# Encoder trunk on one core: weight sums queued behind the normed operands, the mixer's evictions before its third operands, gates without GpSimd

## The chip, the cores and the metric

The kernel runs on one core of a Trainium2 chip. The metric is the device time of one launch in microseconds (us), the median of several runs. Lower is better.

## The reference

Two layers work on one sequence of 512 tokens with 1024 channels, all in float32. Each layer adds half a SwiGLU feed-forward stage, a token mixer and another half feed-forward stage to `x`, each behind an RMS norm:

```
x = x + 0.5 * swiglu(rmsnorm(x), w1_a, w3_a, w2_a)      # (silu(h @ w1) * (h @ w3)) @ w2, 2816 wide
h = rmsnorm(x); p = h @ w_in                            # fourier, B, C, v, pool: 512 each; gates 3 x 1024
x = x + (sig(g_f)*fourier(p_f) + sig(g_c)*conv(p) + sig(g_p)*pool(p_p)) @ w_o
x = x + 0.5 * swiglu(rmsnorm(x), w1_b, w3_b, w2_b)
```

`fourier` is the real part of a two-dimensional Fourier transform over tokens and over groups of 128 channels, followed by a linear map per group. `conv` is a gated convolution of width 3, `pool` a pooling over four window sizes with a linear map per group. A last norm makes the output.

## The kernel before, in words

**Products.** All activations lie transposed: 128 channels on the partitions, 512 tokens in the free dimension, eight such tiles for `x`. Every float32 product is three matmuls (`mm`, L354 to L358): both operands are split into a high and a low part of a reduced type (`h` and `l` at a name's end), and high x high (L356), high x low (L357) and low x high (L358) are added in PSUM. Making such a pair is a copy of the high part, on ScalarE as a rule, and a subtraction for the low part.

**Jobs of seven products.** Gate and up projections, and most of the mixer's input projection, are done as jobs of two output blocks with seven block products instead of eight: M1 to M7, each 4 x 3 matmuls of 256 columns. The activations' operands for them come from `operands(j)` (L452 to L481), called for j = 0 to 3, that is for pairs of `x` tiles. It makes two normed tiles `t` (L457: x times gain times `rstd`), four sums of 256 columns (L463 to L466, made by `tt`, whose instructions stand at L431), copies as high parts (L471, L476) and four low parts `n`. Two low parts are subtractions on VectorE (L478, which also shows as `n<-t,n` at L431). The two others are a negated copy on ScalarE (L473) and a DMA from GpSimd's queue that adds the source on top (L474). M1 needs what L471 and L478 make of the first unit, M5 and M7 the first accumulating DMA's result, M6 and M4 the second's.

**Weights.** `Weights` (L147) streams the weights in, as `Layout` planned it from a dry run: every step has a due time a fixed stretch ahead of its use (`AHEAD`), and is issued when the program's own estimate of time passes it. A load is a DMA on SP's queue (L185) into `raw` (3 buffers), `z` (2) or `w22` (2). For a job, `raw` holds the first blocks, `z` and `w22` the others. The steps are: `raw`, split with an accumulating DMA (L204 to L206); `sums`, two additions of 512 columns (L228, L229) and a split (L191 copy, L192 subtraction); `rest`, a subtraction of 1024 columns (L235) and a split, after which `raw` and `z` are free for the next load; and `last`, a split of `w22`. Subtractions of splits are held back in `tail` and issued by `finish` (L197).

**Stages.** A feed-forward stage begins with `lead` (L592): its first three hidden blocks (four in the first stage) are computed directly from the unscaled `h`, while the norm's factor `rstd` and the operands for the jobs are made; `gate_up` (L441) ends such a block with a multiplication by `rstd` on VectorE, a silu on ScalarE (L444), a second multiplication by `rstd` on GpSimd (`ptt`, L434), the product with the up projection (L431) and a split. The other blocks are jobs, run by `run` (L508), with pieces of the down projection between them.

**The mixer** (`mix`, L803) first does the small products of the Fourier map and the w_in product for the Fourier columns: four sums in PSUM, one per 128 tokens, whose last steps end one after another. `evict` (L822) copies each from PSUM, scaled: `pfh` on ScalarE (L825) and `pfl` on VectorE (L826). The operands 0 to 2 are made at steps 11, 17 and 23 of that loop, the last after it. Then `pf` is multiplied with the tables of the Fourier transform; the eight results are copied out as `half` (L859), four from each of two groups, and their banks in PSUM (eight in all) are used again by the jobs that follow. `join` (L739) combines two halves on VectorE.

**Order.** The program's text gives the order of tracing; the tile framework's scheduler then orders each engine's queue by when things can be ready, with the tracing order as the priority. Every engine works through its queue in that order and waits where its next instruction isn't ready. `tc.issue_after(i)` adds an order without a wait for data: what is traced inside stands behind instruction i in its engine's queue.

Of the kernel before, what the change touches and what calls it, by code (L numbers as in the profile page):

```python
# [1 line left out]

# [1 line left out]

# [6 lines left out]
F32 = mybir.dt.float32  # L11
F32R = mybir.dt.float32r
AF = mybir.ActivationFunctionType
ALU = mybir.AluOpType
# [46 lines left out]
NOTHING = Nothing()  # L61


class Order:


    def __init__(self):
        self.log, self.t = [], 0.0

    def start(self, x):  # L70
        pass
# [75 lines left out]
class Weights:  # L147
# [2 lines left out]

    BUFS = {"raw": 3, "z": 2, "w22": 2, "part": 6, "part22": 1}

    def __init__(self, nc, dram, pool, layout):
        self.nc, self.dram, self.pool, self.plan = nc, dram, pool, layout
        self.at, self.loads, self.splits = 0, list(layout.loads), list(layout.splits)
        self.used = dict.fromkeys(self.BUFS, 0)
        self.raws, self.ready, self.tail, self.t = {}, {}, [], 0.0
# [38 lines left out]

    def finish(self, t):  # L197
        while self.tail and self.tail[0][0] <= t:
            self.tail.pop(0)[2]()

    def added_parts(self, src, key, w=2 * S, tag="part"):

        hi, lo = (self.tile_of(tag, w if tag == "part22" else MAXW, F32R, tag + n) for n in "hl")
        self.nc.scalar.activation(lo[:, :w], src, AF.Copy, scale=-1.0)  # L204
        self.nc.gpsimd.dma_start(lo[:, :w], self.source(key), accum_op=ALU.add)  # L205
        self.nc.scalar.copy(hi[:, :w], src)  # L206
        return hi, lo

    def step(self, kind, key):
        v = self.nc.vector  # L210
# [41 lines left out]
    def advance(self, need):  # L252
        t = self.t = self.plan.log[self.at][2]
        self.finish(t - 1.3)
        while True:
            moved = False
            while self.loads and self.loads[0][0] <= t and self.load():
                moved = True
            while self.splits and self.splits[0][0] <= t and self.step(*self.splits[0][1:]):
                self.splits.pop(0)  # L260
                moved = True
            if not moved:
                break
        while need not in self.ready:
            if self.loads and self.load():
                continue
            assert self.step(*self.splits[0][1:]), (need, self.splits[0], self.used)
            self.splits.pop(0)
        if self.tail and any(made == need for _, made, _ in self.tail):
            self.finish(t)  # L270
# [30 lines left out]
def encoder(ctx: ExitStack, tc: tile.TileContext, layout, x_in, w_in, consts_in, gain_in, out):  # L301
    nc = tc.nc
    const = ctx.enter_context(tc.tile_pool(name="const", bufs=1))
    wpool = ctx.enter_context(tc.tile_pool(name="wpool", bufs=2))
# [1 line left out]
    tmp = ctx.enter_context(tc.tile_pool(name="tmp", bufs=2))  # L306
    psp = ctx.enter_context(tc.tile_pool(name="psp", bufs=8, space=bass.MemoryType.PSUM))

    weights = layout if isinstance(layout, Order) else Weights(nc, w_in, wpool, layout)
    cst = const.tile([P, NCONST[0]], F32, name="cst")  # L310
    nc.scalar.dma_start(cst, consts_in)
    zero = act.tile([P, S], mybir.dt.bfloat16, tag="act", name="zero")
# [47 lines left out]
    def cut(pair, a, b):  # L360
        return pair[0][:, a:b], pair[1][:, a:b]

    state = {}
# [66 lines left out]
    def tt(out, a, b, op=ALU.mult):  # L430
        nc.vector.tensor_tensor(out=out, in0=a, in1=b, op=op)  # L431

    def ptt(out, a, b, op=ALU.mult):
        nc.gpsimd.tensor_tensor(out=out, in0=a, in1=b, op=op)  # L434

    def t32(tag, w=S):

        wide = tag in ("t0", "t1", "t2", "t3")
        return tmp.tile([P, S + 32 if wide else S], F32, tag=tag, name=tag, bufs=1 if wide else 2)[:, :w]

    def gate_up(p1, p3):  # L441
        a = t32("a")
        tt(a, p1, state["r"])
        nc.scalar.activation(a, a, AF.Silu)  # L444
        ptt(a, a, state["r"])
        b = t32("b")
        tt(b, p3, a)
        pair = act_pair("g")
        split_tile(b, *pair)
        return pair  # L450

    def operands(j):  # L452


        w1, w2, z1, z2 = (act.tile([P, AW], F32, tag="act", name="t")[:, :S] for _ in range(4))
        for odd, w in enumerate((w1, w2)):
            nc.vector.scalar_tensor_tensor(  # L457
                out=w, in0=x[2 * j + odd], scalar=state["gain"][2 * j + odd], in1=state["r"],
                op0=ALU.mult, op1=ALU.mult,
            )  # L460

        left, right = slice(0, Q), slice(Q, S)
        tt(z1[:, left], w1[:, right], w1[:, left], ALU.subtract)  # L463
        tt(z1[:, right], w2[:, right], w1[:, right], ALU.subtract)
        tt(z2[:, left], w2[:, right], z1[:, left], ALU.subtract)
        tt(z2[:, right], w2[:, left], z2[:, left], ALU.subtract)  # L466
        units = [act.tile([P, AW], F32R, tag="act", name="n")[:, :S] for _ in range(7)]
        pairs = [units[0:2], units[2:4], units[4:6], (units[6][:, :Q], units[6][:, Q:])]
        sources = [w2, z1, z2, w1[:, left]]
        for i in (3, 0):  # L470
            nc.scalar.copy(pairs[i][0], sources[i])  # L471
        for i in (1, 2):
            nc.scalar.activation(pairs[i][1], sources[i], AF.Copy, scale=-1.0)  # L473
            nc.gpsimd.dma_start(pairs[i][1], sources[i], accum_op=ALU.add)  # L474
        for i in (1, 2):
            nc.scalar.copy(pairs[i][0], sources[i])  # L476
        for i in (3, 0):
            tt(pairs[i][1], sources[i], pairs[i][0].bitcast(F32), ALU.subtract)  # L478
        place = {"M1": (3, 0), "M2": (0, 0), "M3": (0, 1), "M5": (1, 0), "M7": (1, 1), "M6": (2, 0), "M4": (2, 1)}
        ops = {q: cut(pairs[i], h * Q, (h + 1) * Q) for q, (i, h) in place.items()}  # L480
        state.setdefault("n", []).append(ops)  # L481
# [321 lines left out]
    def mix(l, after):  # L803
# [31 lines left out]
        for n, (k, t) in enumerate(order):  # L835
            if n == 5:
                mean_squares(True)
            if n == 9:
                spread(True)
            if n in (11, 17, 23):  # L840
                operands((n - 11) // 6)
            if k == len(ws):
                ws.append(weights.tile(("w_in", l, k * P, 0, S), 4.0 if k < KD - 2 else 2.0, True))
            mm(pss[t], [tokens(part, t, True) for part in h[k]], ws[k], k == 0, k == KD - 1)
            if k == KD - 1:
                evict(t)
        operands(3)

        halves = []
        for g2 in range(0, NG, 2):  # L850
            pss = [psum()[:, : 2 * QC] for _ in range(4)]
            for k in range(2):
                w = weights.tile(("table", 0, k * P, 0, 2 * QC), 2.0, True)
                for j in range(4):
                    g = g2 + j // 2
                    mm(pss[j], cut(pf[2 * k + j % 2], g * P, (g + 1) * P), w, k == 0, k == 1)
            for ps in pss:
                half = act.tile([P, AW], F32, tag="act", name="half")[:, : 2 * QC]
                nc.scalar.copy(half, ps)  # L859
                halves.append(half)  # L860
        v, yf, pooled, conv, merged, zs, ys = {}, {}, {}, {}, {}, {}, {}

        def fourier(m):
# [169 lines left out]
    for l in range(L):  # L1033
        ffn(l, "_a", next_norm("g_mix", l), first=l == 0)
        mix(l, next_norm("g_ffn2", l))
        last = l == L - 1
# [95 lines left out]
```

## Time and profile before

| what | value |
|---|---|
| median of 3 runs | 2077.1 us (2074.5 to 2081.96) |
| the profiled execution | 2079.14 us |
| its span | 2077.3 us |
| its mean granted TensorE clock | 0.994 |
| HBM read | 282.34 MB |

A row of the page's busy times gives engine, busy us, share of the span and count. PE is TensorE's matmuls, PEld its weight loads, DVE VectorE, ACT ScalarE, POOL GpSimd, SP the engine that issues loads. A row of a timeline gives the start and duration in us, engine, line, operation, output and inputs by name, shape and type, a count, and in brackets how long the engine had been idle before and what released it. Rows that run on without a gap on an engine overlap a little at their ends. A row of a window gives the busy time of each engine in that stretch and TensorE's mean granted clock, 1.00 being full speed.

### The profile page before, as it was taken

To read this page: it belongs to the slowest core of one execution; us is meant where nothing else is said; L and a number is where in the kernel's file an instruction comes from. 1 tells how busy PE (TensorE), PEld (TensorE's weight loads), DVE (VectorE), ACT (ScalarE), POOL (GpSimd) and SP (SyncE) were. 2 spreads that over 40 slices of the span, in tenths; PEclk is the share of its full clock that TensorE was granted. 3 is DMA by queue.
4 is the path that set the end of the run, shared out by engine and by line. 5 is a ranking of instruction groups with operands and counts; after the bars stand their busy time and mean duration, and the time that the engine had idled before them with its cause. 6 is when DMAs were issued, how large, how long until landed. Compare 5 with 4: busy or idle time off the path is not lost.

```text
span 2077.3 us, 33989 instructions
## 1 busy us (share of the span) xinstructions
PE 2033.2 (98%) x13590; PEld 1865.7 (90%) x13590; DVE 1357.1 (65%) x2022; ACT 1175.1 (57%) x1847; POOL 266.2 (13%) x321
## 2 busy tenths in 40 slices
PE   8899999899999999999999999998999999999998
PEld 6898998799998898899879899988999987989996
DVE  5764773589876575477367458637898756745752
ACT  6643664676654664465466356547666556635642
POOL 3300001200000410010230000022000023000000
PEclk9999999999999999999999999999999999999999
DMA  8744664745664764466575446557566567634641
GB/s 237 157 143 107 158 173 123 151 123 143 161 159 141 150 155 142 108 157 170 132 144 149 122 126 156 160 126 148 138 161 173 139 157 140 165 112 114 161 138 41
DMA packets 104846, 299.23 MB, mean 144 GB/s; under 512 B 11632, under 2 KB 13040, under 8 KB 104688
## 3 DMA queue, kind: packets, MB, share of 16 engines
q1 hardware_dynamic: 75744, 205.31, 30.3%
q0 software_dynamic: 28800, 91.52, 25.7%
q8 instruction: 106, 1.74, 0.3%
q14 instruction: 52, 0.43, 0.1%
q10 hardware_dynamic: 144, 0.24, 0.0%
HBM read 282.34 MB, written 2.10 MB: 137 GB/s over the span
## 4 chain that ended last, share of the span: by engine, by line
PE 88%; DVE 3%; DMA 3%; ACT 2%; issue 2%; POOL 1%; POOLq 0%; SPq 0%; ACTq 0%; DVEq 0%
PE ps L356 29%; PE ps L357 29%; PE ps L358 29%; DMA raw<-weights 1%; DVE t L457 1%; DVE t L431 1%; DMA n<-t 1%; ACT parth L206 0%; DMA w<-weights 0%; DMA z<-weights 0%; POOL n L474 0%; ACT n L476 0%; DVE raw L235 0%; POOL a L434 0%; DVE n L431 0%
## 5 line engine op out<-in xcount | busy, mean ns | idle before, releaser
L357 PE MATMUL ps<-n,parth 128*128 128x256 f32 x2760 | 779.0, 282 | 12.2 <-DVE n L431 6.2
L356 PE MATMUL ps<-n,parth 128*128 128x256 f32 x2760 | 776.7, 282 | 10.1 <-ACT half L859 5.7
L358 PE MATMUL ps<-n,partl 128*128 128x256 f32 x2760 | 775.9, 281 | 0.0
L357 PEld LDWEIGHTS ps<-n,parth 128*128 128x128 f32 x2760 | 521.7, 189 | 16.0 <-DMA n<-t 7.2
L356 PEld LDWEIGHTS ps<-n,parth 128*128 128x128 f32 x2760 | 521.4, 189 | 13.1 <-ACT half L859 6.1
L358 PEld LDWEIGHTS ps<-n,partl 128*128 128x128 f32 x2760 | 523.0, 189 | 0.0
L192 DVE TENSOR_TENSOR partl<-raw,parth 128x1024 fp32r<-128x1024 f32 (+2 forms) x241 | 285.0, 1186 | 104.8 <-ACT parth L191 104.8
L191 ACT CAST parth<-raw 128x1024 fp32r<-128x1024 f32 (+2 forms) x241 | 243.9, 1013 | 171.5 <-PE ps L357 146.1
L205 POOL DMA_DIRECT2D partl<-weights x152 | 133.9, 881 | 1381.0 <-ACT partl L204 1100.3
L206 ACT CAST parth<-raw 128x1024 fp32r<-128x1024 f32 (+1 forms) x152 | 158.1, 1040 | 182.9 <-PE ps L357 138.6
L356 PE MATMUL ps<-gh,parth 128*128 128x512 f32 x608 | 239.7, 394 | 0.0
L357 PE MATMUL ps<-gl,parth 128*128 128x512 f32 x608 | 239.6, 394 | 0.0
L358 PE MATMUL ps<-gh,partl 128*128 128x512 f32 x608 | 239.5, 394 | 0.0
L523 ACT COPY sM<-ps 128x256 f32<-128x256 f32 x345 | 127.5, 370 | 143.9 <-PE ps L358 142.9
L204 ACT ACTIVATE partl<-raw 128x1024 fp32r<-128x1024 f32 (+1 forms) x152 | 159.6, 1050 | 11.1 <-PE ps L357 7.2
L192 DVE TENSOR_TENSOR partl<-z,parth 128x1024 fp32r<-128x1024 f32 x115 | 140.2, 1219 | 32.8 <-ACT parth L191 32.8
L191 ACT CAST parth<-z 128x1024 fp32r<-128x1024 f32 x115 | 120.9, 1051 | 69.4 <-PE ps L357 46.2
L431 DVE TENSOR_TENSOR b<-ps,sM 128x256 f32<-128x256 f32 x222 | 93.2, 420 | 98.9 <-PE ps L358 98.7
L235 DVE TENSOR_TENSOR raw<-raw,z 128x1024 f32<-128x1024 f32 x115 | 140.7, 1223 | 20.7 <-ACT partl L204 13.6
L191 ACT CAST part22h<-w 128x512 fp32r<-128x512 f32 x115 | 71.3, 620 | 128.0 <-PE ps L357 112.0
L358 PEld LDWEIGHTS ps<-gh,partl 128*128 128x128 f32 x608 | 114.1, 188 | 26.9
L356 PEld LDWEIGHTS ps<-gh,parth 128*128 128x128 f32 x608 | 114.2, 188 | 25.6
(177 smaller groups left out, 3254.4 us busy)
## 6 DMA issues: line engine op xcount, KB each, us to landing
raw<-weights SPq DMA_DIRECT2D x259, 512.0 KB, 4.1
partl<-weights POOLq DMA_DIRECT2D x146, 512.0 KB, 5.5
z<-weights SPq DMA_DIRECT2D x115, 256.0 KB, 2.6
w<-weights SPq DMA_DIRECT2D x115, 256.0 KB, 2.8
n<-t POOLq DMA_DIRECT2D x48, 256.0 KB, 5.3
x<-x_t SPq DMA_DIRECT2D x8, 256.0 KB, 4.7
raw<-weights SPq DMA_DIRECT2D x10, 128.0 KB, 3.4
out<-t SPq DMA_DIRECT2D x4, 256.0 KB, 2.0
```

The costliest lines, as they stand in the source:

```text
L191: self.nc.scalar.copy(hi[:, :w], src)
L192: self.tail.append((self.t, self.made, lambda: self.nc.vector.tensor_tensor(out=lo[:, :w], in0=src, in1=hi[:, :w].bitcast(F32), op=ALU.sub ...
L204: self.nc.scalar.activation(lo[:, :w], src, AF.Copy, scale=-1.0)
L205: self.nc.gpsimd.dma_start(lo[:, :w], self.source(key), accum_op=ALU.add)
L206: self.nc.scalar.copy(hi[:, :w], src)
L235: v.tensor_tensor(out=raw, in0=raw, in1=raws.pop(("third", key))[:, : 2 * S], op=ALU.subtract)
L356: nc.tensor.matmul(ps, ah, bh, start=start, stop=False, skip_group_check=more)
L357: nc.tensor.matmul(ps, ah, bl, start=False, stop=False, skip_group_check=more)
L358: nc.tensor.matmul(ps, al, bh, start=False, stop=stop, skip_group_check=more)
L431: nc.vector.tensor_tensor(out=out, in0=a, in1=b, op=op)
L457: nc.vector.scalar_tensor_tensor(out=w, in0=x[2 * j + odd], scalar=state["gain"][2 * j + odd], in1=state["r"], op0=ALU.mult, op1=ALU.mult,)
L523: nc.scalar.copy(b["s" + q], ps)
```

## The change

Four things are altered.

1. At the end of each `operands(j)` its last low part on VectorE is stored in `weights.behind`. Every weight step traced later (`sums`, `rest`, splits, and what `finish` issues) goes through `queued`, and so stands behind that instruction in its engine's queue.
2. Inside `operands` the instructions are written in another order: the copies of M1's to M3's units come between the sums, the low part for M1 after the third sum, and each accumulating DMA as soon as its source is made. Nothing is added or removed.
3. In the mixer `operands(2)` moves from step 23 of the w_in loop to behind it, and so behind the four evictions; `operands(3)` moves between the two groups of `half` copies.
4. `gate_up` multiplies both projections by `rstd` on VectorE and then one with the other; the multiplication on GpSimd is gone. VectorE has one instruction more per block, for 13 blocks.

The lines have other numbers after the change: L431 (sums, products, low parts) becomes L442 and L478, L457 L468, L471 and L476 L487, L489, L496 and L497, L473 L483, L474 L484, L825 and L826 L846 and L847, L859 L880, L191 L193, L192 L194, L228 and L229 L239 and L240, L235 L246, L336 L347.

```diff
+    def queued(self):
+        return nullcontext() if self.behind is None else self.tc.issue_after(self.behind)
+    def queued_step(self, kind, key):
+        with self.queued():
+            return self.step(kind, key)
     def finish(self, t):
         while self.tail and self.tail[0][0] <= t:
-            self.tail.pop(0)[2]()
+            with self.queued():
+                self.tail.pop(0)[2]()
...
     def gate_up(p1, p3):
         a = t32("a")
+        b = t32("b")
         tt(a, p1, state["r"])
+        tt(b, p3, state["r"])
         nc.scalar.activation(a, a, AF.Silu)
-        ptt(a, a, state["r"])
-        b = t32("b")
-        tt(b, p3, a)
+        tt(b, b, a)
...
-        for i in (3, 0):
-            nc.scalar.copy(pairs[i][0], sources[i])
-        for i in (1, 2):
-            nc.scalar.activation(pairs[i][1], sources[i], AF.Copy, scale=-1.0)
-            nc.gpsimd.dma_start(pairs[i][1], sources[i], accum_op=ALU.add)
-        for i in (1, 2):
-            nc.scalar.copy(pairs[i][0], sources[i])
-        for i in (3, 0):
-            tt(pairs[i][1], sources[i], pairs[i][0].bitcast(F32), ALU.subtract)
+        nc.scalar.copy(pairs[3][0], sources[3])
+        tt(z1[:, left], w1[:, right], w1[:, left], ALU.subtract)
+        nc.scalar.copy(pairs[0][0], sources[0])
+        tt(z1[:, right], w2[:, right], w1[:, right], ALU.subtract)
+        added(1)
+        tt(z2[:, left], w2[:, right], z1[:, left], ALU.subtract)
+        lower(3)
+        tt(z2[:, right], w2[:, left], z2[:, left], ALU.subtract)
+        added(2)
+        nc.scalar.copy(pairs[1][0], sources[1])
+        nc.scalar.copy(pairs[2][0], sources[2])
+        last = lower(0)
+        weights.behind = last if nc is NOTHING else last.ins
...
-            if n in (11, 17, 23):
+            if n in (11, 17):
                 operands((n - 11) // 6)
...
-        operands(3)
+        operands(2)
...
                 halves.append(half)
+            if g2 == 0:
+                operands(3)
```

What this does to the queues shows in three places. The first is VectorE's queue in the mixer of layer 0, from the third operands (made of the tiles x_90 and x_91 of `x`) to the fourth (x_92, x_93). Before:

```order
L457 SCALAR_TENSOR_TENSOR t<-x_90,cst,rstd 128x512
L457 SCALAR_TENSOR_TENSOR t<-x_91,cst,rstd 128x512
L431 TENSOR_TENSOR t<-t 128x256 x3
L228 TENSOR_TENSOR z<-z,w_4198 128x512
L431 TENSOR_TENSOR t<-t 128x256
L431 TENSOR_TENSOR n<-t,n 128x256
L229 TENSOR_TENSOR z<-z,raw 128x512
L192 TENSOR_TENSOR partl<-raw,parth 128x1024
L431 TENSOR_TENSOR n<-t,n 128x512
L826 SCALAR_TENSOR_TENSOR pfl<-ps,rtok,pfh 128x512 x4
L457 SCALAR_TENSOR_TENSOR t<-x_92,cst,rstd 128x512
L457 SCALAR_TENSOR_TENSOR t<-x_93,cst,rstd 128x512
```

After:

```order
L847 SCALAR_TENSOR_TENSOR pfl<-ps,rtok,pfh 128x512 x4
L468 SCALAR_TENSOR_TENSOR t<-x_90,cst,rstd 128x512
L468 SCALAR_TENSOR_TENSOR t<-x_91,cst,rstd 128x512
L442 TENSOR_TENSOR t<-t 128x256 x2
L478 TENSOR_TENSOR n<-t,n 128x256
L442 TENSOR_TENSOR t<-t 128x256 x2
L478 TENSOR_TENSOR n<-t,n 128x512
L442 TENSOR_TENSOR t_4164<-half,cst 128x260
L468 SCALAR_TENSOR_TENSOR t<-x_92,cst,rstd 128x512
L468 SCALAR_TENSOR_TENSOR t<-x_93,cst,rstd 128x512
```

The evictions `pfl` stand ahead of the third operands (x_90, x_91) now, no weight step stands among the operands, and one step of `join` has come ahead of the fourth.

The second place is ScalarE's queue at the same point, from the third operands' copies or the evictions on. Before:

```order
L476 CAST n<-t 128x512 x2
L825 ACTIVATE pfh<-ps,rtok 128x512 x4
L191 CAST parth<-z 128x1024
L471 CAST n<-t 128x256
L471 CAST n<-t 128x512
L473 ACTIVATE n<-t 128x512
L204 ACTIVATE partl<-raw 128x1024
L473 ACTIVATE n<-t 128x512
L476 CAST n<-t 128x512 x2
L859 COPY half<-ps 128x260 x8
```

After:

```order
L846 ACTIVATE pfh<-ps,rtok 128x512 x4
L487 CAST n<-t 128x256
L489 CAST n<-t 128x512
L483 ACTIVATE n<-t 128x512 x2
L496 CAST n<-t 128x512
L497 CAST n<-t 128x512
L880 COPY half<-ps 128x260 x4
L487 CAST n<-t 128x256
L489 CAST n<-t 128x512
L483 ACTIVATE n<-t 128x512
L544 COPY sM_4162<-ps 128x256
```

Before, the evictions stand behind the third operands and the eight `half` copies behind the fourth, with the weights' steps between; after, the evictions come first and four of the `half` copies stand between the third operands and the fourth.

The third place is VectorE's queue in the lead of layer 0's second feed-forward stage, from its fourth operands (x_92, x_93) to the first weight steps behind them. Before:

```order
L192 TENSOR_TENSOR partl<-raw,parth 128x1024
L431 TENSOR_TENSOR n<-t,n 128x512
L235 TENSOR_TENSOR raw<-raw,z 128x1024
L336 TENSOR_TENSOR gl<-b,gh 128x512
L457 SCALAR_TENSOR_TENSOR t<-x_92,cst,rstd 128x512
L457 SCALAR_TENSOR_TENSOR t<-x_93,cst,rstd 128x512
L431 TENSOR_TENSOR t<-t 128x256 x3
L431 TENSOR_TENSOR a<-ps,rstd 128x512
L431 TENSOR_TENSOR t<-t 128x256
L431 TENSOR_TENSOR n<-t,n 128x256
L192 TENSOR_TENSOR partl<-z,parth 128x1024
L431 TENSOR_TENSOR b<-ps,a 128x512
```

After:

```order
L442 TENSOR_TENSOR t<-t 128x256
L442 TENSOR_TENSOR a<-ps,rstd 128x512
L442 TENSOR_TENSOR t<-t 128x256
L442 TENSOR_TENSOR b<-ps,rstd 128x512
L442 TENSOR_TENSOR b<-b,a 128x512
L478 TENSOR_TENSOR n<-t,n 128x512
L246 TENSOR_TENSOR raw<-raw,z 128x1024
L347 TENSOR_TENSOR gl<-b,gh 128x512
L239 TENSOR_TENSOR z<-z,w_7798 128x512
L194 TENSOR_TENSOR partl<-raw,parth 128x1024
L240 TENSOR_TENSOR z<-z,raw 128x512
L194 TENSOR_TENSOR part22l<-w_7499,part22h 128x512
```

The weight steps L246, L239, L240 and L194 stand behind the fourth operands' last low part (L478, 512 columns), where before L192 and L235 stood among and ahead of the operands; the last gate's two multiplications and its product (`a`, `b`) now stand ahead of that low part too.

More of the change, by code (lines that the diff above doesn't have):

```diff
@@ L1 @@
-from contextlib import ExitStack
+from contextlib import ExitStack, nullcontext
 import numpy as np
@@ L67, in __init__ @@
     def __init__(self):
-        self.log, self.t = [], 0.0
+        self.log, self.t, self.behind = [], 0.0, None
     def start(self, x):
@@ L151, with __init__ @@
     BUFS = {"raw": 3, "z": 2, "w22": 2, "part": 6, "part22": 1}
-    def __init__(self, nc, dram, pool, layout):
+    def __init__(self, tc, dram, pool, layout):
+        nc = tc.nc
+        self.tc, self.behind = tc, None
         self.nc, self.dram, self.pool, self.plan = nc, dram, pool, layout
@@ L258, in advance @@
                 moved = True
-            while self.splits and self.splits[0][0] <= t and self.step(*self.splits[0][1:]):
+            while self.splits and self.splits[0][0] <= t and self.queued_step(*self.splits[0][1:]):
                 self.splits.pop(0)
@@ L266, in advance @@
                 continue
-            assert self.step(*self.splits[0][1:]), (need, self.splits[0], self.used)
+            assert self.queued_step(*self.splits[0][1:]), (need, self.splits[0], self.used)
             self.splits.pop(0)
@@ L307, in encoder @@
     psp = ctx.enter_context(tc.tile_pool(name="psp", bufs=8, space=bass.MemoryType.PSUM))
-    weights = layout if isinstance(layout, Order) else Weights(nc, w_in, wpool, layout)
+    weights = layout if isinstance(layout, Order) else Weights(tc, w_in, wpool, layout)
     cst = const.tile([P, NCONST[0]], F32, name="cst")
@@ L462, in operands @@
         left, right = slice(0, Q), slice(Q, S)
[L463 to L466, printed above, removed]
         units = [act.tile([P, AW], F32R, tag="act", name="n")[:, :S] for _ in range(7)]
@@ L469, in operands, with lower, added @@
         sources = [w2, z1, z2, w1[:, left]]
-        for i in (3, 0):
-            nc.scalar.copy(pairs[i][0], sources[i])
-        for i in (1, 2):
+        def lower(i):
+            return nc.vector.tensor_tensor(
+                out=pairs[i][1], in0=sources[i], in1=pairs[i][0].bitcast(F32), op=ALU.subtract
+            )
+        def added(i):
             nc.scalar.activation(pairs[i][1], sources[i], AF.Copy, scale=-1.0)
             nc.gpsimd.dma_start(pairs[i][1], sources[i], accum_op=ALU.add)
-        for i in (1, 2):
-            nc.scalar.copy(pairs[i][0], sources[i])
-        for i in (3, 0):
-            tt(pairs[i][1], sources[i], pairs[i][0].bitcast(F32), ALU.subtract)
+        nc.scalar.copy(pairs[3][0], sources[3])
[11 more added lines that the diff above has]
+        weights.behind = last if nc is NOTHING else last.ins
         place = {"M1": (3, 0), "M2": (0, 0), "M3": (0, 1), "M5": (1, 0), "M7": (1, 1), "M6": (2, 0), "M4": (2, 1)}
```

## The prediction

> **What bounds the kernel now.** I read the page's busy shares first, then TensorE's list of waits, then the granted clock in windows round those waits, then the timelines there. The page, busy us and share by engine:
>
> ```profile
> PE 2033.2 (98%) x13590; PEld 1865.7 (90%) x13590; DVE 1357.1 (65%) x2022; ACT 1175.1 (57%) x1847; POOL 266.2 (13%) x321
> ```
>
> TensorE is the bound, so the change, which removes none of its matmuls, can only win back time in which TensorE waits or runs slowly. What it waits for (us in all, times, longest):
>
> ```profile
> PE ps L356 <- ACT pfh L825: 7.2, 2, 3.6
> PE ps L357 <- DVE n L431: 6.2, 4, 2.1
> PE ps L357 <- DMA n<-t: 6.0, 6, 1.5
> PE ps L356 <- ACT half L859: 5.7, 2, 2.8
> PE ps L356 <- ACT n L471: 2.6, 1, 2.6
> PE ps L356 <- ACT sM L523: 1.8, 2, 1.3
> ```
>
> That is 29.5 us, all of it in six places: where the normed operands (`n`) of a feed-forward stage are made (four leads) and in the two mixers. Windows (from:to, us; busy us of PE, PEld, DVE, ACT, POOL; granted clock) add what the waits drag behind them:
>
> ```profile
> 68.50:71.90 3.40, 3.30 (x15) 3.24 (x16) 3.40 (x5) 3.40 (x7) 3.40 (x4) 0.50 0.42 77
> 404.40:409.80 5.40, 5.40 (x24) 5.32 (x25) 5.40 (x11) 3.93 (x7) 0.00 (x0) 0.50 0.65 151
> 412.90:415.70 2.80, 0.00 (x0) 0.00 (x0) 0.00 (x0) 2.80 (x6) 1.43 (x2) 1.00 0.59 122
> 415.70:420.10 4.40, 4.36 (x24) 4.36 (x25) 3.50 (x11) 3.87 (x11) 0.49 (x3) 0.61 0.99 172
> 1080.00:1091.00 11.00, 6.57 (x50) 5.94 (x49) 7.67 (x14) 7.26 (x11) 3.88 (x4) 1.00 0.81 159
> 1427.00:1430.40 3.40, 2.96 (x13) 2.89 (x14) 3.40 (x6) 2.11 (x4) 0.35 (x1) 0.50 0.96 181
> 1437.30:1440.70 3.40, 2.99 (x14) 2.99 (x15) 2.17 (x8) 2.33 (x10) 0.83 (x3) 0.50 0.96 152
> ```
>
> Busy time times the missing clock is the price: 3.30 x .5 = 1.65 after the first lead's waits, 5.40 x .5 = 2.7 and 4.36 x .39 = 1.7 in mixer 0, 2.96 x .5 = 1.5 and 2.99 x .5 = 1.5 in mixer 1, together 9.0. All that can be won is so 29.5 + 9.0 = 38.5 us. The row at 1080 shows a lead whose stalls did not lower the clock: it was idle for 4.4 of 11 us, but in pieces.
>
> How the time divides: mixer 0 has 3.6 + 2.85 + 2.7 + 1.7 = 10.8; mixer 1 the same waits and 3.0 of clock, 9.4; that leaves 18.3 for the four leads, of which the first has 2.6 + 2.1 + 1.65 and most of the 1.8, some 8.0, and the other three 10.3 together.
>
> **The mixers: order of the evictions.** Timeline of mixer 0 (start, us, engine, line, idle before and its releaser):
>
> ```profile
> 387.35 0.69 DVE L229 TENSOR_TENSOR z<-z,raw 128x512 f32<-128x512 f32 x1 [4.24 <-DMA raw<-weights]
> 394.02 1.22 DVE L235 TENSOR_TENSOR raw<-raw,z 128x1024 f32<-128x1024 f32 x1
> 402.62 1.12 ACT L476 CAST n<-t 128x512 fp32r<-128x512 f32 x2
> 403.65 2.41 ACT L825 ACTIVATE pfh<-ps,rtok 128x512 fp32r<-128x512 f32 x4
> 404.38 0.58 PE L356 MATMUL ps<-parth,pfh 128*128 128x260 f32 x1 [3.61 <-ACT pfh L825]
> 415.32 2.31 ACT L859 COPY half<-ps 128x260 f32<-128x260 f32 x8
> ```
>
> The w_in sums are ready at 404.38 - 3.61 = 400.8, but ScalarE makes the third operands' copies until 403.65, and only then evicts. After the change the four evictions come first on ScalarE and VectorE, so the first table matmul can follow 400.8 by one eviction of 2.41/4 = 0.6; three of the four finish earlier still, since each w_in sum ends at its own time. The 3.61 goes, and with it the half clock behind it (2.7): 6.3 less about 0.5 left.
>
> The price is that the third operands now come after the evictions and the fourth after half of the `half` copies, both nearer to their use. Before, the table products end at about 412.9 and TensorE waits 2.85 for the eight copies of 2.31/8 = 0.29 each, which on ScalarE stand behind the fourth operands' copies and so begin only at 415.32. In the new order four copies stand right behind the third operands; by my walk (new order, durations from these rows) they free the banks at about 407.0 and the first product M1 starts with 0.7 lost. The fourth operands wait for the first `join`, so their accumulating DMA is the last thing due: it lands at about 415.6, when M6 wants it. I add up 3.5 us of stall left in the mixer, in pieces of at most 1.3. Mixer 0 gains 10.8 - 3.5 = 7.3, mixer 1 9.4 - 3.5 = 5.9.
>
> Does the clock still drop? The 3.61 was followed by 0.50, and so was the idle 2.80 at 412.90 (0.61 over the window behind it); the pieces of up to 1.55 at 1080 kept 1.00. So I take no drop under 1.5 and a drop above 2.8. The Trainium skill, "TensorE: Matmul & The Clock Gate" (Part 1: The HAM clock gate, What's actually happening), says the clock falls after at least one idle window of about 3.4 us of a free-running counter. The 2.80 with its 0.61 disagrees with that figure taken as a threshold, so the trace decides; by the page the second drop of each mixer, 1.7 and 1.5, would be no consequence of the wait, could stay, and my sum would be about 3 us smaller.
>
> **Weight steps queue behind the operands.** In the mixer the first operands wait for a weight sum that itself waits 4.24 us for a load (387.35); now they can start when `rstd` is there, about 2.6 us earlier, and L235 (394.02) no longer stands between their sums. In the leads, with the second feed-forward stage of layer 0 as the sample:
>
> ```profile
> 707.08 1.42 DVE L457 SCALAR_TENSOR_TENSOR t<-x,cst,rstd 128x512 f32<-128x512 f32 x2 [3.58 <-ACT rstd L424]
> 716.28 0.69 DVE L228 TENSOR_TENSOR z<-z,w 128x512 f32<-128x512 f32 x1 [1.44 <-DMA z<-weights]
> 720.56 2.45 DVE L457 SCALAR_TENSOR_TENSOR t<-x,cst,rstd 128x512 f32<-128x512 f32 x2
> 726.94 1.21 DVE L235 TENSOR_TENSOR raw<-raw,z 128x1024 f32<-128x1024 f32 x1
> 732.28 1.21 DVE L192 TENSOR_TENSOR partl<-z,parth 128x1024 fp32r<-128x1024 f32 x1
> 731.82 0.86 POOL L474 DMA_DIRECT2D n<-t  x1 [4.93 <-ACT n L473]
> 734.60 0.86 POOL L474 DMA_DIRECT2D n<-t  x1
> 734.68 0.69 DVE L431 TENSOR_TENSOR b<-ps,a 128x512 f32<-128x512 f32 x1 [1.19 <-POOL a L434]
> 735.29 0.68 DVE L431 TENSOR_TENSOR n<-t,n 128x512 fp32r<-128x512 f32 x1
> 729.69 0.39 PE L358 MATMUL ps<-hh,partl 128*128 128x512 f32 x1
> 732.41 0.39 PE L357 MATMUL ps<-n,parth 128*128 128x256 f32 x1 [1.14 <-DVE n L431]
> 737.96 0.39 PE L357 MATMUL ps<-n,parth 128*128 128x256 f32 x1 [1.33 <-DMA n<-t]
> ```
>
> VectorE builds operands from 707.08 to 735.97 (the 512-wide lower at 735.29). Between stand four 1024-wide weight steps of 1.21 and two 512-wide of 0.69 (6.2 us) and a wait of 1.44 for a load. All go behind the last lower. That is not 7.6 us gained on the path: the last gate needs the lead's last sum, which TensorE ends at 730.1 (729.69 + 0.39), so the last lower cannot come before that, its multiplications and the silu between them. I walk it to 733.2 instead of 735.97.
>
> More to the point, the fourth operands' first accumulating DMA (z1) now leaves at about 730.5 rather than 731.82, the second (z2) at 732.3 rather than 734.60. The second landed by 737.96, that is 3.3 after its issue; with that z1 is there at 733.8 and z2 at 735.6. Without stalls TensorE wants z1 at about 733.1 and z2 at 735.8. Left: 0.8 us per lead. But DMAs of this kind vary:
>
> ```profile
> DMA to landing us min/median/max: 3.2/5.3/8.0
> raw<-weights SPq DMA_DIRECT2D x259, 512.0 KB, 4.1
> ```
>
> At the median 5.3 they would be 2.0 late in each lead. I take 3.3, the row of this place, and keep 5.3 for the range. In return, two jobs' weight sums, rests and lowers come later. **Who waits for that:** TensorE for the parts of the first two jobs, and SP, whose loads need the buffers that those steps free. Order and durations put the first rest's lower at 736.6 and the next job's sums at 740.4, and TensorE wants them at about 741.3. I cost this at nothing, but the cover is under 1 us; if it is gone, each us late counts once per seam, six times. For the six seams I allow 2 us.
>
> **Gates leave GpSimd.** The multiplication by `rstd` (L434), and the first lead's wait for it:
>
> ```profile
> L434 POOL TENSOR_TENSOR a<-a,rstd 128x512 f32<-128x512 f32 x13 | 22.8, 1784 | 5.5 <-ACT a L444 5.3
> 60.76 0.69 DVE L431 TENSOR_TENSOR b<-ps,a 128x512 f32<-128x512 f32 x1 [5.92 <-POOL a L434]
> 66.15 0.38 PE L356 MATMUL ps<-n,parth 128*128 128x256 f32 x1 [2.61 <-ACT n L471]
> 68.60 0.58 PE L357 MATMUL ps<-n,parth 128*128 128x256 f32 x1 [2.06 <-DVE n L431]
> ```
>
> GpSimd loses 13 instructions of 1.78; VectorE gains 13 of about 0.69 (the `b` row), 9 us in all, none of it on the path while VectorE waits anyway (the 5.92 alone is more than the first lead's four, 2.8). In the first lead that wait held everything behind it back; without it the walk has the fourth operands' last lower at 62.5, while TensorE came to want them at 66.15 - 2.61 = 63.5. Of that lead's 8.0 I leave 1.0. The gates also slowed VectorE: the two L457 at 720.56, beside a gate, took 2.45 where the pair at 707.08 took 1.42, so 1.0 per gate that falls so. The Trainium skill, "SBUF — State Buffer" (SBUF: two separate sides), calls the ports that VectorE and GpSimd share an exclusive lock, also for a VectorE operation with two SBUF inputs against a GpSimd operation that reads SBUF; the 2.45 agrees.
>
> **The sum**, against the profiled execution (2079.1): mixers 7.3 + 5.9, first lead 7.0, the three other leads 10.3 - 2.4 = 7.9, less 2 for late weights: 26.1. That gives 2053.0; the profiled execution lies 2.0 above the median 2077.1, so against the median 2051.
>
> **Rivals.**
>
> Slower: weights arrive late. The loads that wait for a freed buffer and the lowers of the first two jobs all move some 10 us back. If at each seam one load (4.1 from issue to landing) had to be waited for in full, plus a half-clocked stretch of 1.5, that is 5.6 x 6 = 33.6 instead of the 2 allowed: 2051 + 31.6 = 2083. It decides from (26.1 + 2)/6 = 4.7 us per seam. Against: a job is 7 x 12 = 84 matmuls, and 24 of about the same width took 5.40 at half clock, so a job gives 84 x 0.11 = 9 us at full clock, while VectorE's weight steps of a job (three of 1.21, three of 0.69) take 5.7 and catch up. For: cover under 1 us.
>
> Smaller gain: the mixers stay tight. If the third and fourth operands' DMAs take 5.3 instead of 3.3, one wait per mixer passes 2.8 and the clock drops again (2 + 1.7 each, 7.4), and the three leads lose 2.0 each (6): gain 12.7, 2064.
>
> Fuller gain: everything but 2 us goes, 36.5: 2041.
>
> No change: the scheduler picks by readiness, and the stalls stay because the rows of the new order wait for the same things. Against: the order of VectorE and ScalarE does change at each of the six places. 2077.
>
> **How the numbers follow.** Forecast 0.55, smaller gain 0.20, fuller 0.12, no change 0.08, slower 0.05. The range 2038 to 2067 takes in the first three (0.87) with some 3 us outside their times. About 0.3%, 6 us, is what a measurement of this kernel can tell from no change: faster 0.87, same 0.08, slower 0.05.
>
> **What would show it.** Right: in the list of TensorE's waits the `pfh` entry gone or under 1 us, `half` under 1.5, no entry for the lowers above 1; the clock at 1.00 in both mixers; the accumulating DMA of `n` as the largest entry left. Wrong: a new entry for a weight part (`parth`, `partl` or a load) in the 10 us behind a seam, granted clock 0.50 after the tables, or the first gate's wait still there under another name.

## The result and the profile after

The changed kernel takes 2059.27 us (median of 4 runs, 2058.85 to 2059.68) against 2077.89 us for the kernel before (median of 4): a ratio of 0.9906, 95% interval 0.9892 to 0.992, 18.6 us less. The profiled execution has a span of 2057.9 us, 19.4 less than before. The forecast was 2051, with 2038 to 2067 as its range: the direction holds, the size is 0.7 of the forecast, and the time lies nearer to the rival "smaller gain" (2064) than to the forecast itself.

TensorE's list of waits in the changed kernel (us in all, times, longest) shows which entries went and which are new:

```profile
PE ps L368 <- DMA n<-t: 7.8, 8, 3.0
PE ps L367 <- ACT sM L544: 3.6, 3, 2.0
PE ps L367 <- ACT parth L193: 2.8, 2, 2.5
PE ps L369 <- DMA partl<-weights: 2.4, 2, 1.8
PE ps L367 <- ACT half L880: 1.9, 2, 0.9
```

The waits for `pfh` (7.2) and for the operands' low parts on VectorE (6.2) are gone, `half` fell from 5.7 to 1.9. But the operands' accumulating DMAs cost more than before (7.8 for 6.0), with one wait of 3.0. The `sM` entry, 1.8 before and all of it in the first lead, is 3.6 now, and 3.4 of that lies in the mixers. The entries for `parth` (L193) and 1.8 us of that for `partl` are waits in the first 45 us, which the kernel before had too.

Stalls and half-clocked stretches together can be read from the starts of the matmuls: each step from one matmul's start to the next, less the median step of its shape in the kernel before, summed over the same stretch of the matmul sequence. In us, for all kernels of this study ("leads" are the three after the first; the kernels other than before and after are described under The experiments). Each column runs up to the next one's place, so that the five together cover the run, and small delays in between are counted with them. Each row is one profile. Executions of one kernel differ by 1 to 4 us, those of the kernel before by up to 8, so a us or two in a column tells little.

| kernel | start, to 45 us | first lead | mixer 0 | leads | mixer 1 | all |
|---|---|---|---|---|---|---|
| before | 10.1 | 9.4 | 12.0 | 13.6 | 10.3 | 55.3 |
| after | 9.5 | 7.1 | 7.3 | 3.1 | 8.9 | 36.0 |
| no_queue | 14.6 | 0.4 | 11.1 | 9.9 | 10.8 | 46.8 |
| scratch2 | 9.7 | 2.4 | 8.0 | 3.1 | 10.0 | 33.2 |
| mix_free | 8.7 | 7.5 | 10.1 | 2.2 | 11.5 | 40.1 |
| old_gates | 10.7 | 10.5 | 8.3 | 11.2 | 8.7 | 49.5 |
| old_mixer | 10.8 | 5.6 | 4.8 | 4.5 | 4.9 | 30.6 |
| old_operands | 10.5 | 5.6 | 9.3 | 1.0 | 10.1 | 36.4 |
| join_late | 13.3 | 0.8 | 8.2 | 3.0 | 9.2 | 34.4 |
| mix_q2 | 9.8 | 3.0 | 9.0 | 4.6 | 10.2 | 36.5 |
| gates_only | 9.8 | 8.8 | 10.5 | 8.1 | 11.9 | 49.0 |
| queue_only | 9.3 | 9.2 | 3.8 | 6.9 | 4.2 | 33.2 |
| queue_gates | 10.4 | 3.5 | 4.2 | 1.2 | 5.0 | 24.4 |
| best | 10.6 | 0.3 | 4.7 | 4.5 | 4.1 | 24.1 |

From before to after the six seams gain 18.9 of the 19.4 us: 10.5 in the three leads, 6.1 in the mixers, 2.3 in the first lead. Two places fell short of the forecast, the mixers and the first lead, and the profile shows what stands there.

**The mixers** end with a wait that was not there before. ScalarE, VectorE and TensorE near 430 us, in mixer 0, in timelines of the changed kernel:

```profile
425.20 0.69 DVE L240 TENSOR_TENSOR z<-z,raw 128x512 f32<-128x512 f32 x1
425.93 1.05 ACT L193 CAST parth<-z 128x1024 fp32r<-128x1024 f32 x1 [2.24 <-DVE z L240]
427.50 1.05 ACT L211 ACTIVATE partl<-raw 128x1024 fp32r<-128x1024 f32 x1
429.39 0.36 ACT L544 COPY sM<-ps 128x256 f32<-128x256 f32 x1
429.80 0.39 PE L367 MATMUL ps<-n,part22h 128*128 128x256 f32 x1 [2.02 <-ACT sM L544]
```

ScalarE's split of `z` waits 2.24 us for a weight sum that VectorE reaches late. Behind it in ScalarE's queue stand more weight steps and then the copy `sM`, which TensorE needs for its bank. TensorE waits 2.0 us for a copy of 0.36.

**The first lead.** GpSimd's queue and TensorE's wait, from the timelines of the changed kernel:

```profile
57.01 0.88 POOL L484 DMA_DIRECT2D n<-t  x1 [0.41 <-issue]
59.53 0.89 POOL L484 DMA_DIRECT2D n<-t  x1 [1.65 <-issue]
60.80 0.88 POOL L484 DMA_DIRECT2D n<-t  x1 [0.37 <-issue]
62.85 0.87 POOL L484 DMA_DIRECT2D n<-t  x1 [1.18 <-ACT n L483]
64.20 0.87 POOL L484 DMA_DIRECT2D n<-t  x1 [0.47 <-ACT n L497]
...
67.51 0.58 PE L368 MATMUL ps<-n,parth 128*128 128x256 f32 x1 [2.96 <-DMA n<-t]
```

The last DMAs leave at 62.85 and 64.20 although their sources, two activations (L483) that ScalarE does from 61.11 to 62.26, are done by then; `issue` in the brackets stands for a wait whose end the profile does not show. In the trace every issue here comes 0.3 us after the landing of the third DMA before it (landings at 56.70, 59.23, 60.48, 62.55 and 63.88). Three are under way at most.

### The profile page after: what moved, and what is told of

It reads as the page before. It is cut to its first block, busy times and chain, and to the rows that moved or that the text cites. A ratio compares the mean times of both kernels' runs of the same rounds, so it can differ in the third digit from the quotient of the medians.

```text
span 2057.9 us, 33977 instructions
## 1 busy us (share of the span) xinstructions
PE 2030.5 (99%) x13590; PEld 1862.4 (90%) x13590; DVE 1359.5 (66%) x2035; ACT 1173.2 (57%) x1847; POOL 245.0 (12%) x308
## 3 DMA queue, kind: packets, MB, share of 16 engines
q1 hardware_dynamic: 75744, 205.31, 30.6%
## 4 chain that ended last, share of the span: by engine, by line
PE 88%; issue 3%; ACT 3%; DVE 2%; DMA 2%; POOL 1%; POOLq 0%; ACTq 0%; DVEq 0%
PE ps L367 29%; PE ps L368 29%; PE ps L369 29%; DMA raw<-weights 1%; DMA n<-t 1%; POOL n L484 1%; DVE t L442 1%; ACT partl L211 1%; DVE partl L194 0%; ACT parth L213 0%; PE ps L409 0%; DMA partl<-weights 0%; DVE t L468 0%; ACT n L483 0%; ACT n L489 0%
## 5 line engine op out<-in xcount | busy, mean ns | idle before, releaser
L194 DVE TENSOR_TENSOR partl<-raw,parth 128x1024 fp32r<-128x1024 f32 (+2 forms) x241 | 285.2, 1187 | 104.5 <-ACT parth L193 104.2
L193 ACT CAST parth<-raw 128x1024 fp32r<-128x1024 f32 (+2 forms) x241 | 244.3, 1014 | 169.3 <-PE ps L368 142.4
L193 ACT CAST parth<-z 128x1024 fp32r<-128x1024 f32 x115 | 121.1, 1053 | 78.8 <-PE ps L368 45.3
L194 DVE TENSOR_TENSOR partl<-z,parth 128x1024 fp32r<-128x1024 f32 x115 | 140.3, 1220 | 33.1 <-ACT parth L193 33.1
L442 DVE TENSOR_TENSOR b<-ps,sM 128x256 f32<-128x256 f32 x222 | 93.2, 420 | 89.8 <-PE ps L369 89.3
L246 DVE TENSOR_TENSOR raw<-raw,z 128x1024 f32<-128x1024 f32 x115 | 140.6, 1223 | 16.5 <-ACT partl L211 13.7
L193 ACT CAST part22h<-w 128x512 fp32r<-128x512 f32 x115 | 71.4, 621 | 116.0 <-PE ps L368 94.0
L368 PEld LDWEIGHTS ps<-gl,parth 128*128 128x128 f32 x608 | 114.2, 188 | 25.6
```

Of the source, the lines that this page charges most:

```text
L194: self.tail.append((self.t, self.made, lambda: self.nc.vector.tensor_tensor(out=lo[:, :w], in0=src, in1=hi[:, :w].bitcast(F32), op=ALU.sub ...
L246: v.tensor_tensor(out=raw, in0=raw, in1=raws.pop(("third", key))[:, : 2 * S], op=ALU.subtract)
L368: nc.tensor.matmul(ps, ah, bl, start=False, stop=False, skip_group_check=more)
```

## The experiments

All times are medians; the ratio is against the kernel before in runs on the same chip. The medians of the kernel before lay between 2076.9 and 2078.2 in these runs, so the differences in us between two experiments are uncertain by about 1 us.

| kernel | us | ratio, 95% interval |
|---|---|---|
| no_queue | 2070.9 | 0.9966 (0.9953 to 0.9978) |
| scratch2 | 2056.7 | 0.9899 (0.9884 to 0.9913) |
| mix_free | 2064.2 | 0.9939 (0.9924 to 0.9954) |
| old_gates | 2073.1 | 0.9978 (0.9968 to 0.9987) |
| old_mixer | 2051.7 | 0.9880 (0.9866 to 0.9895) |
| old_operands | 2060.5 | 0.9918 (0.9903 to 0.9932) |
| join_late | 2058.0 | 0.9909 (0.9893 to 0.9926) |
| mix_q2 | 2059.5 | 0.9915 (0.9900 to 0.9930) |
| gates_only | 2073.7 | 0.9981 (0.9971 to 0.9991) |
| queue_only | 2056.4 | 0.9897 (0.9882 to 0.9912) |
| queue_gates | 2050.1 | 0.9865 (0.9850 to 0.9880) |
| best | 2048.9 | 0.9862 (0.9847 to 0.9877) |

**no_queue**: part 1 undone.

```diff
-        weights.behind = last if nc is NOTHING else last.ins
```

> The changed kernel with weights.behind never set, so the weight steps are ordered by readiness again; the new operand order, the mixer's new order and the gates on VectorE stay. My theory now: queueing saved the stalls of three leads (they lost 3.2, 4.9 and 3.5 us before and 0.7, 0.3 and 0.8 after) but costs 2.2 + 3.0 us behind the mixers, where VectorE's weight steps come late (TensorE's waits of 2.0 and 1.4 for sM, and a half-clocked 3.4 us). Then without it the leads lose some 2 us each again and the mixers' late waits go: 2059 + 6 - 5 = 2060, no clear change. Rival, queueing carries the whole change: 2068 or more. Second rival, queueing is worth nothing in the leads, since the gates did it: 2054.

2070.9, the rival's side: without queueing 11.6 us are lost. The mixers lose 5.7 of stall and half clock (11.1 + 10.8 against 7.3 + 8.9), the leads 6.8; the start loses 5.1, and the first lead wins 6.7. The late wait for `sM` did go, as I expected, but far more came back: `half` at 5.7 us and half-clocked stretches.

**scratch2**: more room for GpSimd's descriptors.

```diff
-    nc = bacc.Bacc("TRN2", ..., dynamic_dma_scratch_size=1024)
+    nc = bacc.Bacc("TRN2", ..., dynamic_dma_scratch_size=2048)
```

> The changed kernel with twice the scratch for GpSimd's DMA descriptors (2048 for 1024); every engine's order is the same. Theory: in the first lead GpSimd issues a DMA only 0.3 us after the third one before it has landed (48.09 after 47.84, 57.01 after 56.70, 64.20 after 63.88), so three are under way at most, and the last accumulating DMA leaves at 64.20 though its source is ready at 62.2. With more room it leaves at 62.4 or earlier and the 3.0 us wait at 64.3 and the half clock behind it (2.7 us) go: 2059 - 5 = 2054. Rival, the transfers themselves are what is slow there (4.4 to 5.5 us each while the DMA engines are nearly full), and more of them at once only make each slower: 2059.

The first lead falls from 7.1 to 2.4, as the theory had it. GpSimd issues the last two DMAs one right behind the other (timeline of scratch2):

```profile
61.56 1.77 POOL L484 DMA_DIRECT2D n<-t  x2 [3.71 <-ACT n L483]
```

The rival happened too, without deciding: the four issued from 49.91 to 56.98 take 7 to 10 us from issue to landing, where those of the changed kernel took 4.4 to 5.5. But the last two land at 65.14 and 67.31, where they landed at 67.46 and 68.81.

The whole gains only 2.6 us. In this profile mixer 0 has 3.4 us at half clock where the changed kernel has none, and mixer 1 has 6.8 where that has 3.4; at half of TensorE's busy time there, that is 1.7 and 1.3 us more, with nearly the same waits (more on that below).

**mix_free**: queueing in the leads only.

```diff
+        if not state.get("free"):
             weights.behind = last if nc is NOTHING else last.ins
...
     def mix(l, after):
         h = take_h()
+        state["free"], weights.behind = True, None
```

> The changed kernel with queueing in the leads only: the mixers' operands do not set weights.behind, and it is cleared at a mixer's start. Theory: the waits of 2.0 and 1.4 us for sM some 24 us into each mixer come from weight steps pushed back behind the mixer's operands (ScalarE's split of z waits for the sum L240, and the copy sM stands behind it on ScalarE); they and one half-clocked stretch go, 2059 - 5 = 2054, while the operands come up to 1 us later per mixer, so 2054 to 2056. Rival, the copies of half and the joins that moved cause these waits: they stay, and the operands come later too: 2059 to 2062.

The late waits for `sM` go, so queueing in the mixers is what makes them, but the kernel is 4.9 us slower. Weight steps stand among the third operands again, on VectorE and, in this timeline of mix_free, on ScalarE, and the copies of `half` behind those are late:

```profile
397.95 1.05 ACT L193 CAST parth<-raw 128x1024 fp32r<-128x1024 f32 x1
399.60 1.05 ACT L193 CAST parth<-z 128x1024 fp32r<-128x1024 f32 x1
401.61 0.41 ACT L487 CAST n<-t 128x256 fp32r<-128x256 f32 x1 [0.95 <-DVE t L468]
404.42 1.06 ACT L211 ACTIVATE partl<-raw 128x1024 fp32r<-128x1024 f32 x1 [0.84 <-PE ps L368]
406.93 1.20 ACT L883 COPY half<-ps 128x260 f32<-128x260 f32 x4
```

TensorE waits 2.8 us for them in each mixer, where it waited 0.9 in the changed kernel. So queueing in the mixers brings more than its late sums cost.

**old_gates**: part 4 undone.

```diff
+        ptt(a, a, state["r"])
-        tt(b, p3, state["r"])
-        tt(b, b, a)
+        tt(b, p3, a)
```

> The changed kernel with the gate's second multiplication by rstd on GpSimd again. Theory: VectorE waits for GpSimd in the leads (5.9 and 1.2 us in the traces of before) and the last low part stands behind that wait, so each of the four leads loses 1 to 2 us: 2063 to 2067. Rival, the wait is hidden now that no weight step stands among the operands: 2059 to 2060.

2073.1, 13.8 us lost, more than either side had. The leads lose 8.1, the first lead 3.4, the rest is spread over start, mixers and small steps. With the operands and the mixer in the old order the same gates are worth 6.3 us (queue_only to queue_gates, below); which of the two new orders doubles that was not tried.

**old_mixer**: part 3 undone.

```diff
-            if n in (11, 17):
+            if n in (11, 17, 23):
...
-        operands(2)
+        operands(3)
...
-            if g2 == 0:
-                operands(3)
```

> The changed kernel with the mixer in the old order: third operands at step 23 of the w_in loop, fourth ahead of the table products; queueing, the new order inside the operands and the new gates stay. Theory: the waits for pfh (3.6) and half (2.8) with their half-clocked stretches come back wholly or in good part, since ScalarE has the copies of the third and fourth operands ahead again; the waits for sM 24 us into the mixers and the waits for the fourth operands' DMA shrink. Each mixer loses 2 to 4 us against the changed kernel: 2063 to 2067. Rival, without weight steps among the operands these come so much earlier that the old place of the evictions costs nothing: 2057 to 2060.

2051.7: 7.5 us faster than the changed kernel, beyond even the rival. The mixer's new order costs time: in the table above the mixers fall from 16.2 to 9.7. ScalarE, VectorE and TensorE in mixer 0 of old_mixer:

```profile
396.05 0.61 ACT L497 CAST n<-t 128x512 fp32r<-128x512 f32 x1
396.56 2.41 ACT L846 ACTIVATE pfh<-ps,rtok 128x512 fp32r<-128x512 f32 x4
399.92 1.40 DVE L468 SCALAR_TENSOR_TENSOR t<-x,cst,rstd 128x512 f32<-128x512 f32 x2
403.65 1.22 DVE L246 TENSOR_TENSOR raw<-raw,z 128x1024 f32<-128x1024 f32 x1
405.15 0.39 PE L367 MATMUL ps<-n,parth 128*128 128x256 f32 x1 [1.49 <-ACT half L880]
```

And VectorE in the changed kernel at the same place:

```profile
404.58 0.43 DVE L442 TENSOR_TENSOR t<-half,cst 128x260 f32<-128x260 f32 x1 [1.72 <-ACT half L880]
404.93 1.41 DVE L468 SCALAR_TENSOR_TENSOR t<-x,cst,rstd 128x512 f32<-128x512 f32 x2
410.22 1.22 DVE L246 TENSOR_TENSOR raw<-raw,z 128x1024 f32<-128x1024 f32 x1
```

Without weight steps among the operands the third ones are done at 396.7, and the evictions start at 396.6 although they stand behind them. TensorE waits under 0.1 us for `pfh`. The fourth operands start at 399.9 instead of 404.9, since the third ones are done earlier and they need not wait for a `join` and its `half`, and the weight steps behind them start at 403.65 instead of 410.22. That takes away TensorE's waits for the fourth operands' DMAs, much of the wait for `sM`, and the half clock. The new order wins 0.56 us at one point (`half`, 0.93 for 1.49). Part 3 is two moves, that of the third operands and that of the fourth; they were undone together, so what each costs alone is not known.

**old_operands**: part 2 undone, with `last` kept for the queueing.

```diff
-        nc.scalar.copy(pairs[3][0], sources[3])
-        tt(z1[:, left], w1[:, right], w1[:, left], ALU.subtract)
...
+        for i in (3, 0):
+            last = nc.vector.tensor_tensor(
+                out=pairs[i][1], in0=sources[i], in1=pairs[i][0].bitcast(F32), op=ALU.subtract
+            )
```

> The changed kernel with the old order of copies, sums and low parts inside the operands. Theory: the order matters where the fourth operands are late, in M1's low part, by about 1 us per lead and mixer: 2062 to 2066. Rival, the scheduler sorts these instructions by readiness anyway, and the engines' queues come out nearly the same: 2059 to 2060.

2060.5, close to the rival: no difference that these runs can tell (2057.2 to 2061.5 against 2058.9 to 2059.7). The leads are better without the new order (1.0 for 3.1), the mixers worse (19.4 for 16.2).

**join_late**: scratch2, and the joins queued like the weight steps.

```diff
-            later.append(lambda g=g: join(halves[2 * g], halves[2 * g + 1], v[g]))
+            later.append(lambda g=g: behind(lambda: join(halves[2 * g], halves[2 * g + 1], v[g])))
```

> The kernel of scratch2 with the mixer's joins queued behind the fourth operands on VectorE. In the changed kernel VectorE is idle for 1.7 us because a join's first step, which needs a half, stands ahead of the fourth operands. Theory: the fourth operands come 1.7 us earlier, and TensorE's two waits for their accumulating DMA (0.7 and 1.0 us in each mixer) go: 2056.7 - 3.5 = 2053, plus or minus 1.5 per half-clocked stretch. Rival, what comes later instead is the joins' result, which the Fourier products need before the first M4: the time moves there, 2056 to 2059.

2058.0, the rival: nothing won. In mixer 0 the first DMA wait went, the second grew to 1.9, and waits for `sM` of 0.5 and 1.4 came behind it, up to 411 and 414.

**mix_q2**: scratch2, and the mixer's weight steps behind the third operands only.

```diff
             if g2 == 0:
+                third = weights.behind
                 operands(3)
+                weights.behind = third
```

> The kernel of scratch2 with the weight steps in the mixers queued behind the third operands only, not behind the fourth. Theory: the first job's rest (L246) fills VectorE's idle 1.7 us, the sums that ScalarE waits for come earlier, so the waits for sM (2.7 us in the two mixers) go; the fourth operands lose little: 2056.7 - 2.5 = 2054. Rival, what is gained there is lost at the fourth operands' DMA, as weight steps stand among the fourth operands again: 2057 to 2060.

2059.5, the rival again: the waits for `sM` late in the mixers went, and the two DMA waits of each mixer became one, of 3.1 and 2.8 us, with 6.8 us at half clock from the midst of it on in both mixers.

**gates_only, queue_only, queue_gates**: the kernel before with part 4, part 1, or both; the edits are those of the change.

> The kernel before with only the gates moved to VectorE. Theory from the runs so far: gates and queueing need each other, since VectorE's last low part waited for both GpSimd and the weight steps; the gates alone bring what no_queue brought, 2071 (2069 to 2073). Rival, the gates are the chief part and the rest of the change took some of it back: 2063 or less.

> The kernel before with only the weight steps queued behind the operands. Theory: the mixers win 11 of their 22 us of stall, as in old_mixer, but the leads keep waiting for GpSimd, and the weight steps behind those waits are later still: 2066 (2062 to 2070). Rival, the late weight steps take back what the mixers win: 2074 to 2078.

> The kernel before with queueing and the new gates, without the new order in the operands and without the mixer's new order. Theory: these two parts make the whole gain, the operands' order is worth under 2 us and the mixer's order costs 7: 2052 (2050 to 2055). Rival, the new order in the operands is needed where the mixer is in the old order: 2056 to 2060.

The gates alone bring 3.6 us, a little less than the theory had (2073.7 for 2069 to 2073), and the waits for `pfh` stay. Queueing alone brings 20.9, more than the whole change; my 2066 for it was wrong, as I had the leads lose more behind GpSimd. The mixers fall to 3.8 and 4.2 with their old order. ScalarE and TensorE in mixer 0 of queue_only, from the third operands' last copies on:

```profile
397.19 1.12 ACT L487 CAST n<-t 128x512 fp32r<-128x512 f32 x2
398.22 2.40 ACT L839 ACTIVATE pfh<-ps,rtok 128x512 fp32r<-128x512 f32 x4
398.94 0.39 PE L367 MATMUL ps<-parth,pfh 128*128 128x260 f32 x1
```

The evictions stand behind the third operands as in the kernel before, and the first table matmul follows without a wait. Both together make 2050.1, as expected, 9 us better than the change as it stands. Against this kernel, old_operands has the mixer's new order alone added: it is 10.4 us slower, a second measure of what part 3 costs.

**best**: old_mixer with the scratch of scratch2.

> The kernel of old_mixer with twice the scratch for GpSimd's DMA descriptors, so that queueing, gates and operand order stand, the mixer keeps its old order, and more than three of GpSimd's DMAs can be under way. Theory: the two gains add, 2051.7 - 3 = 2049 (2047 to 2051). Rival, what the first lead gains goes into its start again (more waiting for the first weights): 2051 to 2053.

2048.9 as expected, 10.4 us below the changed kernel; against queue_gates (2050.1) it is no clear step. Its list of waits has little of the seams left (the 2.8 for `partl` lies in the first 45 us):

```profile
...
PE ps L367 <- ACT half L880: 2.9, 2, 1.5
PE ps L369 <- DMA partl<-weights: 2.8, 1, 2.8
PE ps L367 <- ACT sM L544: 1.3, 4, 0.4
PE ps L368 <- DMA n<-t: 1.3, 3, 0.6
```

## Why the prediction was right in direction, and where its steps failed

- **The bound** was read rightly: only waits and half clock at the seams could be won, and 18.9 of 19.4 us came from there.
- **The three leads**: forecast 7.9, measured 10.5; the table counts 13.6 there before the change, where the prediction had 10.3, since it also counts small delays that the list of waits leaves out. The walk held: accumulating DMAs that land 3.3 after issue (722.83 and 724.58, 3.3 each) and stalls of 0.7 to 0.8 in two leads, 0.3 in the third.
- **The mixers, size**: forecast 13.2, measured 6.1. The walk up to the first M4 held, 3.6 of stall in mixer 0 for 3.5. Left in the two mixers are 16.2 where the forecast left 7.0. The step that cost late weights at 2 us for all seams failed: the waits for `sM` alone cost 2.2 and 1.6 there. Half clock in mixer 1 adds 1.7, and the rest is in delays of under 0.3 us each. I had named TensorE and SP as those who wait, and not ScalarE, whose queue carries the copies that free PSUM.
- **The mixers, cause**: this is the step that was wrong. I put the end of the `pfh` wait down to the evictions' new place. The waits for `pfh` came from weight steps among the operands before them: queue_only ends them in the old order, gates_only keeps 6.8 us of them, and old_mixer shows the new order as a loss of 7.5 us. With the old order kept, the mixers gain 12.6 (22.3 to 9.7), about what I had forecast for the new one. The new place ends these waits too (no_queue, without queueing, has none in its list), but I had credited one part with a wait that another part ends by itself.
- **The clock**: "no drop under 1.5" failed. In mixer 1 two waits for the DMAs, of 0.76 and 1.06, brought the clock to 0.50; in mixer 0 nearly the same two (0.71 and 0.97) did not.
- **The first lead**: forecast 7.0, measured 2.3. VectorE's wait for GpSimd went as forecast, the last low part came at 61.9 (walk: 62.5). The step that failed was to walk the low parts alone and leave the accumulating DMAs out, as if each were issued once its source is ready and landed in time. The first of the last two left some 1.1 us after its source was ready and took 4.6 to land, and TensorE waited 2.96 for it. scratch2 shows that the limit of three made most of this.
- **The gates**: right that they leave a wait on the path; costed within the leads only. Alone they bring 3.6, on top of queueing 6.3.
- **Rivals**: the late weights of the first rival happened, at 1.6 to 2.2 us, in the mixers only, far from the 4.7 per seam at which it would have decided. "Smaller gain" had the clock drop again in the mixers (it did in one) and DMAs at 5.3 us there, where they took 3.3 to 3.7.
- **The signs**: `pfh` gone, no entry for the low parts and the accumulating DMA as the largest entry came as said. `half` is 0.9 in each mixer, but 1.9 as an entry where the sign was 1.5, and the clock stayed at 1.00 in mixer 0 only; the 0.50 in mixer 1 was named as a sign of being wrong.
- **Luck**: that the time lies in the range owes something to errors of opposite sign. The mixers gained 7.1 less than forecast and the first lead 4.7 less, the three leads gained 2.6 more, the start 0.6 that was not foreseen, and the 2 set aside for late weights are part of the mixers' shortfall. The gain of part 1 hid that part 3 lost time.

## What to carry to other kernels

When a change has several parts at one place, cost each part also as if the others had already been made: the evictions were late only because of work that another part took away, and moving them then just delayed what came next. When steps are pushed back on one engine, walk every in-order queue that consumes them, ScalarE's here, and look for short copies that stand behind a waiting one. And where a queue's DMAs leave later than their data is ready, compare each issue with the landings before it.

## What the runs showed of the hardware

**The clock's windows.** In all profiles of this study the granted clock changes on a grid of 3.41 us. Three windows of the changed kernel on that grid at full clock, in mixer 0, mixer 1 and mixer 0, the second with the one behind it, in which the clock fell (from:to, us; busy PE, PEld, DVE, ACT, POOL; clock, DMA share, GB/s):

```profile
411.30:414.70 3.40, 2.28 (x16) 2.07 (x17) 3.15 (x6) 2.53 (x5) 0.00 (x0) 1.00 0.67 142
...
1421.60:1425.00 3.40, 1.78 (x12) 1.58 (x13) 3.40 (x6) 2.40 (x6) 0.00 (x0) 1.00 0.68 154
1425.00:1428.40 3.40, 3.40 (x19) 3.40 (x18) 2.79 (x6) 2.59 (x3) 0.40 (x1) 0.50 0.51 155
428.30:431.70 3.40, 1.90 (x16) 1.90 (x17) 3.40 (x14) 2.42 (x5) 1.01 (x3) 1.00 0.67 126
```

Idle time adds up within a window: 1.6 idle of 3.4, in two pieces, brought the clock to 0.50 for the next window; 1.1 and 1.5 in the two others did not. Over the 14 profiles, from 20 us on and short of the kernel's end, all 27 full-speed windows with 1.84 us or more idle were followed by half clock, 17 of 54 with 1.20 to 1.83, and none with less. At half clock it stayed there behind windows with 0.62 us or more idle, and rose behind all with less. The Trainium skill, "TensorE: Matmul & The Clock Gate" (Part 1: The HAM clock gate, What's actually happening), has a free-running window of about 3.4 us, and the grid agrees; its condition, at least one idle window, does not, as 1.84 idle of 3.41 was enough each time. So one and the same stall can cost a half-clocked window or nothing by where the grid falls: half of TensorE's busy time in it, at most 1.7 us. This is how scratch2 and the changed kernel differ in their mixers.

**GpSimd's DMAs.** In the first lead of the changed kernel, with the scratch at 1024, a fourth DMA waits for the landing of the first; with 2048 up to six were under way there (in scratch2 at 51.90).

**Open** stays why the start costs 14.6 us in no_queue and 13.3 in join_late against 8.7 to 10.8 in the others. In no_queue it shows as 10.2 us at half clock from 34.3 on, in join_late as a wait of 3.9 for a weight part's DMA and 6.8 us at half clock. Open is also what between 1.20 and 1.83 us of idle decides on the clock.
